# Seven block products instead of eight in the down projections of a two-layer decoder trunk

## The chip, the core and the metric

The kernel runs as one program on one core of a Trainium2 chip. Its time is in device microseconds for one execution; three runs are shown, and their median is the number that is compared. The profile comes from one further execution. Its engines are TensorE (PE, with its weight loads PEld), VectorE (DVE), ScalarE (ACT), GpSimd (POOL) and SyncE (SP, which here issues the loads).

## What is computed

The reference is a trunk of two layers over a residual stream x of 256 tokens by 1024 columns, float32. Each layer has a mixer (attention) and then a feed-forward network (FFN), and a last RMSNorm ends it. The change touches the FFNs alone:

```python
def swiglu(h, w_gate, w_up, w_down):
    return (jax.nn.silu(h @ w_gate) * (h @ w_up)) @ w_down

x = x + swiglu(rmsnorm(x, norm_ffn[layer]), ffn_w_gate[layer], ffn_w_up[layer], ffn_w_down[layer])
```

The gate and up matrices are 1024 x 2816, the down matrix is 2816 x 1024. The down projection multiplies 256 x 2816 values by it.

## The kernel before

**Number format.** Every float32 operand of a matmul is split into a high part, rounded to the format that PE multiplies (fp32r), and a low part, the rest. ACT makes the high part by a copy, DVE the low part by a subtraction. A product is three matmuls: high by high, high by low, low by high (mm3, L361).

**Weights.** The class Weights (L73) holds one queue of all weight tiles in the order of use. A tile of a down projection is one k-tile: 128 rows of the matrix by all 1024 columns, 512 KB. `load` issues its DMA on SP's queue into one of four raw buffers, `prepare` (L98) splits it into one of seven pairs of high and low buffers (L111 on ACT, L114 on DVE), and `next` (L118) hands out a tile and prepares up to six tiles ahead. A split must wait until the matmuls that read the buffer seven tiles earlier are done.

**FFN.** `ffn` (L468) first runs the gate and up projections in eleven chunks of 256 hidden units (L490). A chunk uses four weight tiles, two for the gate and two for the up projection; weights are the stationary operand, the activations of all 256 tokens the moving one (L503 with the weights' high parts, L505 with their low parts). The gate sums lie in two of four PSUM banks with the tag mm, the up sums in the two banks with the tag s, so that the next chunk's up projection needs the banks of the last one. Then, for each of the chunk's two blocks of 128 units (L510 to L520): the gate sums are copied and added, scaled and put through silu in a tile `sg` (three buffers); the up sums are copied to `hn` (L517 on ACT) and added (L518 on DVE), multiplied by `sg` (L519) and split into the tiles `hh` and `hl` (L520, by way of the helper at L247). These hold all 22 k-tiles of hidden values until the down projection ends.

**Down projection.** `residual` (L382) runs over the 22 k-tiles. Here the hidden values are the stationary operand, 128 x 128, and the weights the moving one, 128 x 512. For each k-tile there are two token blocks t by two column halves h, each with three matmuls: 12 matmuls, summed in four banks of tag mm (`ps_out`). The last three k-tiles are kept back and done block by block (L405, L406), so that the first sums are finished early: DVE scales each block by the token's normalization factor and adds it to x (L448), and the next layer's norm (`Norm.half`, L278) multiplies, has PE transpose (L254, in the two banks of tag tp) and splits. In the second layer the final norm follows instead (`Final`, L314).

**Order.** Each engine runs its instructions in an order that is fixed when the program is built: a scheduler goes through them by the order of the source and by when it reckons them ready. SP's loads are held in source order. The next layer's first weight tiles are split during the end of a down projection, in the same queue.

Of the kernel before, what the change touches and what calls it, by code (L numbers as in the profile page):

```python
# [7 lines left out]
F32 = mybir.dt.float32  # L8
# [21 lines left out]
OD_CHUNKS = [304, 256, 512, 512, 512, 512]  # L30
FF_CHUNKS = [256] * 11
WCOLS = 1024


def in_tiles(chunks):
# [37 lines left out]
class Weights:  # L73


    def __init__(self, tc, pool, rpool, flats, specs, ahead, bufs, spare):
        self.tc, self.pool, self.rpool, self.ahead, self.bufs, self.spare = tc, pool, rpool, ahead, bufs, spare
        self.queue = []
        for flat, tiles in zip(flats, specs):
            off = 0  # L80
            for kk, w in tiles:
                n = kk * w
                self.queue.append((flat[off : off + P * n].rearrange("(p c) -> p c", p=P), kk, w))
                off += P * n
        self.raw = []
        self.ready = []
        self.parts = []
        self.used = 0
        self.later = 0

    def load(self, upto):
        while len(self.raw) < min(upto, len(self.queue)):
# [5 lines left out]
    def prepare(self, upto, behind=False):  # L98

        nc = self.tc.nc  # L100
        while len(self.ready) < min(upto, len(self.queue)):
            i = len(self.ready)
            self.load(i + 1)
            raw = self.raw[i]
            self.raw[i] = None
            _, kk, w = self.queue[i]
            n = kk * w
            hi = self.pool.tile([P, WCOLS], F32R, tag="hi", bufs=self.bufs[1], name="w_hi")
            lo = self.pool.tile([P, WCOLS], F32R, tag="lo", bufs=self.bufs[1], name="w_lo")
            with self.tc.high_priority(offset=-self.later):  # L110
                act = nc.scalar.activation(hi[:, :n], raw[:, :n], AF.Copy)  # L111
                if behind:
                    self.tc.keep_in_program_order(act)
                sub = nc.vector.tensor_sub(lo[:, :n], raw[:, :n], hi[:, :n])  # L114
                self.parts.append((act, sub))
            self.ready.append((hi[:, :n].rearrange("p (k c) -> p k c", k=kk), lo[:, :n].rearrange("p (k c) -> p k c", k=kk)))

    def next(self, hold=1):  # L118
        i = self.used
# [7 lines left out]
def trunk(tc, x, w0, w1, sm0, cw, vec, gcol, cst, out, dbg=None):  # L127
# [251 lines left out]
                nm.finish()  # L379
        return ps  # L380

    def residual(act, nk, tail, nxt, rs=None, amid=None, gate=(), hold=False):  # L382

        ps = [[mm_bank("ps_out") for _ in range(2)] for _ in range(NT)]
        inorder = amid is not None and not hold
# [1 line left out]
        def one(t, h, k, wt):  # L387
            c = slice(512 * h, 512 * h + 512)
            skip = isinstance(nxt, Final) and (t, h) == (NT - 1, 1)
            return mm3(ps[t][h], act[t], k, wt[0][:, 0, c], wt[1][:, 0, c], k == 0, k == nk - 1 - skip * tail, skip)  # L390

        for k in range(nk - tail):
            wt = W.next()
            for t in range(NT):
                for h in range(2):
                    one(t, h, k, wt)
        last = [W.next(hold=tail) for _ in range(tail)]
        if amid and not hold:
            order = [(t, h, 0, tail) for t, h in ((0, 0), (0, 1), (1, 0), (1, 1))]
# [68 lines left out]
    def ffn(nm, goff):  # L468
        wide, rs = nm.wide, nm.rs
        nxt = Final() if goff == V_FIN else Norm(goff)  # L470
        with tc.tile_pool(name="ffn", bufs=1, side="left", reuse_waits="tile") as fp:
            hh = fp.tile([P, KF, T], F32R, tag="hh", name="hT_hi")
            hl = fp.tile([P, KF, T], F32R, tag="hl", name="hT_lo")


            ones = fp.tile([P, P], F32, tag="ones", name="ones")
# [13 lines left out]
            for w in FF_CHUNKS:  # L490
# [4 lines left out]
                for dst in (gp, up):  # L495
# [11 lines left out]
                        nm.finish()  # L507
                    if dst is gp and f0 == 0:
                        spread()
                for f in range(nf):  # L510
                    sg = fp.tile([P, T], F32, tag="sg", bufs=3, name="sg")
                    hn = fp.tile([P, T], F32, tag="hn", bufs=3, name="hn")
# [4 lines left out]
                    evac(hn, up[f][:, T:])  # L517
                    V.tensor_add(hn, up[f][:, :T], hn)  # L518
                    V.tensor_mul(hn, hn, sg)  # L519
                    split(hh[:, f0 + f], hl[:, f0 + f], hn)  # L520
                f0 += nf
                if f0 == 3 * nf:
                    gain(goff)
            hT = [[z[:, :, t * P : (t + 1) * P] for z in (hh, hl)] for t in range(NT)]
            residual(hT, KF, 3, nxt, rs)
        return nxt


# [639 lines left out]
```

## Time and profile before

| what | us |
|---|---|
| median of three runs (lowest, highest) | 652.33 (651.77, 652.62) |
| the profiled execution | 652.22 |
| its span, first to last instruction | 650.4 |
| first FFN, first gate matmul in the chain that ended last | 137.97 |
| first FFN, first matmul of the down projection | 261.34 |
| second FFN, first gate matmul in the chain that ended last | 460.06 |
| first split of a down tile that waits for the second down projection's matmuls | 589.00 |

In the page, PE is 88% of the chain that ended last. The three lines of mm3 in the down projections (L363, L364, L365 with `ps_out`) have 176 matmuls each with hidden values as the stationary operand. A matmul's length in the records (389 ns on average for 128 x 512) is longer than the distance of one to the next, since they are pipelined; the distance is read from the starts. A line with a helper's number (L111, L114, L220, L247) collects the calls of many places, so that they are told apart by the names of their tiles and by their shape.

### The profile page before, as it was taken

The numbers are of one execution on the slowest core, as the hardware profiler recorded it, in microseconds if no ns is written. First come the engines' busy times: TensorE is split into PE (matmuls) and PEld (weight loads), VectorE is DVE, ScalarE is ACT, GpSimd is POOL, SyncE is SP. The second block draws the span as 40 slices with busy tenths as digits, with TensorE's granted clock in tenths as the row PEclk, the third lists the DMA queues.
The fourth block names the chain that finished last, engine by engine and source line by source line (L and its number), as shares of the span: only waits on it lengthen the run. The fifth ranks groups of instructions, "written<-read, shape, count | busy, mean of one in ns | idle before, by whom it ended". The sixth has DMA issues, their size and how long they took to land.

```text
span 650.4 us, 10025 instructions
## 1 busy us (share of the span) xinstructions
PE 638.9 (98%) x3521; PEld 537.5 (83%) x3521; DVE 478.9 (74%) x1116; ACT 403.0 (62%) x809; POOL 11.0 (2%) x26
## 2 busy tenths in 40 slices
PE   8999999999999999999999999999999999999995
PEld 5978888888888888888888877776888888888884
DVE  6999976678867677544589889797887777765424
ACT  6685748558665665433377597787676665564314
POOL 2000000100000000000000000000000000000000
PEclk9999999999999999999999999999999999999998
DMA  8834354218755655564186511402286555556501
GB/s 302 295 128 153 98 172 154 97 53 287 244 194 194 193 187 190 183 194 151 49 328 234 188 67 56 171 34 93 85 283 234 190 187 187 183 185 210 191 14 66
DMA packets 31729, 109.02 MB, mean 168 GB/s; under 512 B 3648, under 2 KB 3904, under 8 KB 31424
## 3 DMA queue, kind: packets, MB, share of 16 engines
q1 hardware_dynamic: 31104, 107.79, 49.3%
q10 hardware_dynamic: 576, 0.59, 0.3%
q8 instruction: 28, 0.46, 0.3%
q14 instruction: 21, 0.17, 0.1%
HBM read 107.32 MB, written 1.05 MB: 167 GB/s over the span
## 4 chain that ended last, share of the span: by engine, by line
PE 88%; ACT 4%; DVE 4%; DMA 2%; issue 1%; SPq 0%; POOL 0%; ACTq 0%; DVEq 0%
PE ps_g L503 12%; PE ps_u L503 12%; PE ps_out L364 8%; PE ps_out L365 8%; PE ps_out L363 8%; PE ps_u L505 6%; PE ps_g L505 6%; PE ps_in L364 5%; PE ps_in L365 5%; PE ps_in L363 5%; PE pt_p L998 2%; PE ps_o L1014 2%; PE ps_s L978 1%; DVE w_lo L114 1%; ACT e L466 1%
## 5 line engine op out<-in xcount | busy, mean ns | idle before, releaser
L114 DVE TENSOR_TENSOR w_lo<-w_raw,w_hi 128x1024 fp32r<-128x1024 f32 (+5 forms) x200 | 231.5, 1179 | 112.6 <-ACT w_hi L111 67.7
L111 ACT ACTIVATE w_hi<-w_raw 128x1024 fp32r<-128x1024 f32 (+5 forms) x200 | 203.4, 1025 | 135.5 <-PE ps_out L365 53.4
L503 PE MATMUL ps_u<-aW,w_hi 128*128 128x512 f32 x352 | 84.9, 391 | 0.0
L503 PE MATMUL ps_g<-aW,w_hi 128*128 128x512 f32 x352 | 84.5, 391 | 0.0
L364 PE MATMUL ps_in<-w_lo,aW 128*128 128x512 f32 (+5 forms) x208 | 77.2, 371 | 0.1
L363 PE MATMUL ps_in<-w_hi,aW 128*128 128x512 f32 (+5 forms) x208 | 76.8, 370 | 0.1
L365 PE MATMUL ps_in<-w_hi,aW 128*128 128x512 f32 (+5 forms) x208 | 75.5, 363 | 0.0
L503 PEld LDWEIGHTS ps_g<-aW,w_hi 128*128 128x128 f32 x352 | 64.6, 188 | 13.1 <-DVE aW L247 0.7
L503 PEld LDWEIGHTS ps_u<-aW,w_hi 128*128 128x128 f32 x352 | 64.4, 188 | 12.2
L364 PE MATMUL ps_out<-w_lo,hT_hi 128*128 128x512 f32 (+1 forms) x176 | 68.3, 388 | 0.0
L363 PE MATMUL ps_out<-w_hi,hT_hi 128*128 128x512 f32 (+1 forms) x176 | 68.3, 388 | 0.0
L365 PE MATMUL ps_out<-w_hi,hT_lo 128*128 128x512 f32 (+1 forms) x176 | 68.3, 388 | 0.0
L505 PEld LDWEIGHTS ps_u<-aW,w_lo 128*128 128x128 f32 x352 | 45.4, 191 | 1.9
L505 PEld LDWEIGHTS ps_g<-aW,w_lo 128*128 128x128 f32 x352 | 45.4, 191 | 1.9
L505 PE MATMUL ps_g<-aW,w_lo 128*128 128x256 f32 x352 | 46.0, 283 | 0.0
L505 PE MATMUL ps_u<-aW,w_lo 128*128 128x256 f32 x352 | 46.0, 283 | 0.0
L466 ACT ACTIVATE e<-e,bias 128x128 f32<-128x128 f32 (+1 forms) x96 | 42.4, 446 | 1.3 <-DVE bias L465 0.9
L364 PEld LDWEIGHTS ps_in<-w_lo,aW 128*128 128x128 f32 x208 | 39.3, 189 | 4.6 <-issue 0.5
L363 PEld LDWEIGHTS ps_in<-w_hi,aW 128*128 128x128 f32 x208 | 39.2, 189 | 4.7 <-ACT w_hi L111 0.3
L365 PEld LDWEIGHTS ps_in<-w_hi,aW 128*128 128x128 f32 x208 | 39.2, 188 | 4.6 <-issue 0.5
L365 PEld LDWEIGHTS ps_out<-w_hi,hT_lo 128*128 128x128 f32 x176 | 33.1, 188 | 6.8
L363 PEld LDWEIGHTS ps_out<-w_hi,hT_hi 128*128 128x128 f32 x176 | 33.1, 188 | 6.7
(237 smaller groups left out, 874.7 us busy)
## 6 DMA issues: line engine op xcount, KB each, us to landing
w_raw<-in_w SPq DMA_DIRECT2D x176, 512.0 KB, 3.8
w_raw<-in_w SPq DMA_DIRECT2D x8, 384.0 KB, 4.5
gain<-in_vec SPq DMA_DIRECT2D x4, 512.0 KB, 5.4
cw<-in_cw SPq DMA_DIRECT2D x2, 1024.0 KB, 7.0
w_raw<-in_w SPq DMA_DIRECT2D x4, 416.0 KB, 5.2
w_raw<-in_w SPq DMA_DIRECT2D x4, 328.0 KB, 5.1
w_raw<-in_w SPq DMA_DIRECT2D x4, 304.0 KB, 2.7
x<-in_x SPq DMA_DIRECT2D x4, 256.0 KB, 5.0
```

The costliest lines, as they stand in the source:

```text
L111: act = nc.scalar.activation(hi[:, :n], raw[:, :n], AF.Copy)
L114: sub = nc.vector.tensor_sub(lo[:, :n], raw[:, :n], hi[:, :n])
L363: TE.matmul(ps, act[0][:, k], wh, start=start, stop=False, skip_group_check=skip),
L364: TE.matmul(ps, act[0][:, k], wl, start=False, stop=False, skip_group_check=skip),
L365: TE.matmul(ps, act[1][:, k], wh, start=False, stop=stop, skip_group_check=skip),
L466: return low, A.activation(e, e, AF.Exp, scale=-1.0, bias=bias, accum_out=den)
L503: TE.matmul(dst[f], wt[0][:, i, f * P : (f + 1) * P], wide[:, k].rearrange("p z q -> p (z q)"), start=k == 0, stop=False)
L505: TE.matmul(dst[f][:, :T], wt[1][:, i, f * P : (f + 1) * P], wide[:, k, 0], start=False, stop=k == KD - 1)
L978: mmi = TE.matmul(sb[:, i], qS[t][:, h], kz[:, par, :, :ns], start=z == 0, stop=z == 1)
L998: TE.transpose(pt[:, i, b, st], e[:, i, b, st * P : (st + 1) * P], ident)
L1014: pin(TE.matmul(ob[64 * par : 64 * par + 64], vv[:, st, c : c + 64], pTs[par][:, b, st].rearrange("p j c -> p (j c)"), start=False, stop=l ...
```

## The change

The hidden values and the down weights of two neighbouring k-tiles are taken as a product of two 2 x 2 block matrices: A is two token blocks by two k-tiles, B is two k-tiles by two column halves. In five of the eleven pairs (FAST: pairs 0, 2, 4, 6 and 8) the four result blocks are formed from seven block products instead of eight (the scheme of Strassen and Winograd), each still three matmuls.

- In the gate and up projections, the chunks of these pairs (a chunk of 256 units is a pair) make four sums of blocks of hidden values (`seven_units`), 128 x 128 each, in two tiles of the tag `sg`, and split these and three of the four blocks. `hh` and `hl` grow from 22 x 256 to 7552 columns, and are addressed by a table.
- `Weights.pair` takes two raw tiles, splits three of the four blocks (half of the first tile, all of the second), and makes four differences of 128 x 512 in two raw sum tiles. `Weights.close` splits the two sum tiles into buffers of their own, two for high and two for low parts. For the first pair of a layer this is done at once, in `pair`; for each further one after the matmuls of the pair before it (`seven` calls `W.close()`). A pair is prepared when both of its tiles are within the distance of six.
- `seven` does the 21 matmuls of a pair. Three products go straight into banks of `ps_out`, four into banks of their own: two of tag tp, two of tag s. The fourth bank of `ps_out` gets nothing from the fast pairs.
- After the last fast pair (k-tiles 16 and 17) the four extra sums are combined and added to x, scaled, by one copy on ACT and six operations on DVE, two of them 1024 columns wide. The ordinary k-tiles 18 to 21 follow.

The core of the diff:

```diff
 WCOLS = 1024
+FAST = (0, 2, 4, 6, 8)
...
         self.later = 0
+        self.pairs = {}
+        self.sums = None
+        self.open = None
...
             i = len(self.ready)
+            if i in self.pairs:
+                if i + 2 > upto:
+                    break
+                self.pair(i)
+                continue
             self.load(i + 1)
...
+    def halves(self, hi, lo, src):
+        act = self.tc.nc.scalar.activation(hi, src, AF.Copy)
+        return act, self.tc.nc.vector.tensor_sub(lo, src, hi)
+    def pair(self, i):
+        V = self.tc.nc.vector
+        self.load(i + 2)
+        a, b = self.raw[i : i + 2]
+        self.raw[i : i + 2] = [None] * 2
+        sums = [self.sums.tile([P, WCOLS], F32, tag="ts", bufs=2, name="w_sum") for _ in range(2)]
+        h = slice(0, 512), slice(512, 1024)
+        got = {}
+        for n, (names, src) in enumerate((((("b11",), a), (("b21", "b22"), b)))):
+            hi = self.pool.tile([P, WCOLS], F32R, tag="hi", bufs=self.bufs[1], name="w_hi")
+            lo = self.pool.tile([P, WCOLS], F32R, tag="lo", bufs=self.bufs[1], name="w_lo")
+            c = slice(0, 512 * len(names))
+            self.parts.append(self.halves(hi[:, c], lo[:, c], src[:, c]))
+            for j, name in enumerate(names):
+                got[name] = (hi[:, h[j]], lo[:, h[j]])
+        V.tensor_sub(sums[0][:, h[0]], a[:, h[1]], a[:, h[0]])
+        V.tensor_sub(sums[0][:, h[1]], b[:, h[1]], a[:, h[1]])
+        V.tensor_sub(sums[1][:, h[0]], b[:, h[1]], sums[0][:, h[0]])
+        V.tensor_sub(sums[1][:, h[1]], b[:, h[0]], sums[1][:, h[0]])
+        self.ready += [got, None]
+        if self.open is None:
+            self.open = (got, sums)
+            self.close()
+        else:
+            self.open = (got, sums)
+    def close(self):
+        if self.open:
+            got, sums = self.open
+            for j, names in enumerate((("t1", "t3"), ("t2", "t4"))):
+                hi = self.sums.tile([P, WCOLS], F32R, tag="thi", bufs=2, name="w_shi")
+                lo = self.sums.tile([P, WCOLS], F32R, tag="tlo", bufs=2, name="w_slo")
+                self.halves(hi, lo, sums[j])
+                for n, name in enumerate(names):
+                    c = slice(512 * n, 512 * n + 512)
+                    got[name] = (hi[:, c], lo[:, c])
+            self.open = ()
+    def both(self):
+        i = self.used
+        self.used += 2
+        self.prepare(i + 2 + self.ahead)
+        got = self.ready[i]
+        self.ready[i] = None
+        return got
     def next(self, hold=1):
...
-    def residual(act, nk, tail, nxt, rs=None, amid=None, gate=(), hold=False):
+    def residual(act, nk, tail, nxt, rs=None, amid=None, fast=(), seven=None, gate=(), hold=False):
...
             skip = isinstance(nxt, Final) and (t, h) == (NT - 1, 1)
-            return mm3(ps[t][h], act[t], k, wt[0][:, 0, c], wt[1][:, 0, c], k == 0, k == nk - 1 - skip * tail, skip)
-
-        for k in range(nk - tail):
+            first = 2 * (0 in fast and t == 1 and h == 1)
+            return mm3(ps[t][h], act[t], k, wt[0][:, 0, c], wt[1][:, 0, c], k == first, k == nk - 1 - skip * tail, skip)
+        k = 0
+        while k < nk - tail:
+            if k in fast:
+                seven(ps, k)
+                k += 2
+                continue
             wt = W.next()
             for t in range(NT):
                 for h in range(2):
                     one(t, h, k, wt)
+            k += 1
         last = [W.next(hold=tail) for _ in range(tail)]
...
         with tc.tile_pool(name="ffn", bufs=1, side="left", reuse_waits="tile") as fp:
-            hh = fp.tile([P, KF, T], F32R, tag="hh", name="hT_hi")
-            hl = fp.tile([P, KF, T], F32R, tag="hl", name="hT_lo")
+            at, sums_at, o = {}, {}, 0
+            for k in range(0, KF, 2):
+                if k // 2 in FAST:
+                    at[0, k], at[0, k + 1], at[1, k + 1], sums_at[k] = o, o + P, o + 2 * P, o + 3 * P
+                    o += 7 * P
+                else:
+                    for i in range(2):
+                        for t in range(NT):
+                            at[t, k + i] = o + (NT * i + t) * P
+                    o += 4 * P
+            hh = fp.tile([P, o], F32R, tag="hh", name="hT_hi")
+            hl = fp.tile([P, o], F32R, tag="hl", name="hT_lo")
+            W.sums = fp
+            W.open = None
+            down = W.used + 2 * KD // ff_kk(FF_CHUNKS[0]) * len(FF_CHUNKS)
+            W.pairs = {down + 2 * g for g in FAST}
+            class Units:
+                def __init__(self, z, t):
+                    self.z, self.t = z, t
+                def __getitem__(self, c):
+                    o = at[self.t, c[1]]
+                    return self.z[:, o : o + P]
+            def seven_units(k, hn):
+                ss = [fp.tile([P, 2, P], F32, tag="sg", bufs=3, name="h_sum") for _ in range(2)]
+                a11, a21, a12, a22 = (hn[i][:, t * P : (t + 1) * P] for i in range(2) for t in range(NT))
+                V.tensor_add(ss[0][:, 0], a21, a22)
+                V.tensor_sub(ss[0][:, 1], ss[0][:, 0], a11)
+                V.tensor_sub(ss[1][:, 0], a11, a21)
+                V.tensor_sub(ss[1][:, 1], a12, ss[0][:, 1])
+                o = at[0, k]
+                split(hh[:, o : o + P], hl[:, o : o + P], a11)
+                split(hh[:, o + P : o + 3 * P], hl[:, o + P : o + 3 * P], hn[1])
+                o = sums_at[k]
+                for i in range(2):
+                    c = slice(o + 2 * i * P, o + 2 * (i + 1) * P)
+                    split(hh[:, c], hl[:, c], ss[i].rearrange("p s q -> p (s q)"))
+            made = {}
+            def seven(ps, k):
+                if not made:
+                    for n in (5, 7):
+                        made[n] = t_bank(f"ps_p{n}")
+                    for n in (6, 1):
+                        made[n] = s_bank(f"ps_p{n}")
+                first, last, begin = k == 2 * FAST[0], k == 2 * FAST[-1], k == 0
+                w = W.both()
+                o = sums_at[k]
+                terms = (
+                    (made[5], o, "t1", first, last),
+                    (made[7], o + 2 * P, "t3", first, last),
+                    (ps[1][0], at[1, k + 1], "t4", begin, False),
+                    (made[6], o + P, "t2", first, last),
+                    (made[1], at[0, k], "b11", first, last),
+                    (ps[0][0], at[0, k + 1], "b21", begin, False),
+                    (ps[0][1], o + 3 * P, "b22", begin, False),
+                )
+                for dst, o, name, start, stop in terms:
+                    u = [z[:, o : o + P].unsqueeze(1) for z in (hh, hl)]
+                    mm3(dst, u, 0, *w[name], start, stop)
+                W.close()
+                if last:
+                    ua = W.sums.tile([P, 2, 512], F32, tag="ts", bufs=2, name="c_sum")
+                    ub = W.sums.tile([P, 2, 512], F32, tag="ts", bufs=2, name="c_sum")
+                    evac(ua[:, 0], made[6])
+                    V.tensor_add(ua[:, 0], made[1], ua[:, 0])
+                    V.scalar_tensor_tensor(xs[0][:, :512], made[1], rs[0], xs[0][:, :512], op0=ALU.mult, op1=ALU.add)
+                    V.tensor_add(ua[:, 1], made[5], ua[:, 0])
+                    V.scalar_tensor_tensor(xs[0][:, 512:], ua[:, 1], rs[0], xs[0][:, 512:], op0=ALU.mult, op1=ALU.add)
+                    V.tensor_add(ub, made[7].unsqueeze(1).broadcast_to([P, 2, 512]), ua)
+                    V.scalar_tensor_tensor(xs[1], ub.rearrange("p a c -> p (a c)"), rs[1], xs[1], op0=ALU.mult, op1=ALU.add)
...
                         spread()
+                hns = []
                 for f in range(nf):
...
                     V.tensor_mul(hn, hn, sg)
-                    split(hh[:, f0 + f], hl[:, f0 + f], hn)
+                    hns.append(hn)
+                    if f0 // nf not in FAST:
+                        o = at[0, f0 + f]
+                        split(hh[:, o : o + T], hl[:, o : o + T], hn)
+                    elif f:
+                        seven_units(f0, hns)
                 f0 += nf
                 if f0 == 3 * nf:
                     gain(goff)
-            hT = [[z[:, :, t * P : (t + 1) * P] for z in (hh, hl)] for t in range(NT)]
-            residual(hT, KF, 3, nxt, rs)
+            hT = [[Units(z, t) for z in (hh, hl)] for t in range(NT)]
+            residual(hT, KF, 3, nxt, rs, fast={2 * g for g in FAST}, seven=seven)
         return nxt
```

## The prediction

> **What bounds the kernel now.** I read the page's engine line first, then the clock row, then the busy time by stages of the FFNs, then single instructions where the stages meet. In the stage rows the columns are the stretch, its length, and busy time with instruction counts of PE, PEld, DVE, ACT, POOL; then granted clock and DMA. The first three are gate and up projections of the first FFN (the two of 11.13 us are its last two chunks), the next two its down projection, the last one the down projection of the second.
>
> ```profile
> PE 638.9 (98%) x3521; PEld 537.5 (83%) x3521; DVE 478.9 (74%) x1116; ACT 403.0 (62%) x809; POOL 11.0 (2%) x26
> PEclk9999999999999999999999999999999999999998
> ...
> 161.31:239.24 77.93, 77.93 (x449) 68.89 (x449) 57.81 (x101) 48.26 (x87) 0.00 (x0) 1.00 0.62 203
> 239.24:250.37 11.13, 11.13 (x66) 9.84 (x65) 8.14 (x15) 6.79 (x13) 0.00 (x0) 1.00 0.55 190
> 250.37:261.50 11.13, 11.13 (x66) 9.84 (x65) 8.14 (x15) 6.79 (x13) 0.00 (x0) 1.00 0.56 189
> ...
> 272.40:283.40 11.00, 11.00 (x51) 9.09 (x50) 4.90 (x4) 4.31 (x5) 0.00 (x0) 1.00 0.60 191
> ...
> 305.40:316.00 10.60, 10.60 (x49) 8.77 (x47) 3.87 (x5) 2.55 (x4) 0.00 (x0) 1.00 0.37 106
> 627.40:638.40 11.00, 11.00 (x50) 9.13 (x49) 1.09 (x2) 0.34 (x1) 0.00 (x0) 1.00 0.01 1
> ```
>
> PE is busy 98% of 650.4 us, at the full granted clock, and in each of these stretches it is busy for the whole length: in the FFNs nothing but PE ends last. DVE has 11.13 - 8.14 = 2.99 us free per chunk of the gate and up projections and 11.00 - 4.90 = 6.1 us in 11.00 us of the down projection. So a matmul removed there is worth its spacing, as long as DVE and ACT deliver the operands.
>
> The spacing: a matmul record's own length overlaps the next one, so I take the beat of a whole k-tile (12 matmuls). In the down projection each high-part split waits for PE to free a buffer, and so beats with it.
>
> ```profile
> 589.00 1.06 ACT L111 ACTIVATE w_hi<-w_raw 128x1024 fp32r<-128x1024 f32 x1 [1.30 <-PE ps_out L365]
> 591.72 1.06 ACT L111 ACTIVATE w_hi<-w_raw 128x1024 fp32r<-128x1024 f32 x1 [1.66 <-PE ps_out L365]
> ...
> 624.36 1.06 ACT L111 ACTIVATE w_hi<-w_raw 128x1024 fp32r<-128x1024 f32 x1 [1.66 <-PE ps_out L365]
> ```
>
> From 589.00 to 624.36 there are 13 k-tiles: 35.36 / 13 = 2.72 us each, 2.72 / 12 = 0.2267 us a matmul.
>
> **The change, part by part.**
>
> *Matmuls removed.* A pair of k-tiles has 2 x 4 x 3 = 24 matmuls before and 7 x 3 = 21 after, all of the same 128x512 shape. Five pairs, two layers: 30 matmuls fewer, 30 x 0.2267 = 6.80 us, all of it on PE's path.
>
> The Trainium skill prices this otherwise: its page TensorE: Matmul & The Clock Gate, section Back-to-back issue gap, gives about 131 ns per matmul of 512 columns in a sustained stream with weight loads. By that the saving would be 30 x 0.131 = 3.9 us, as an estimate, and the sum below 2.9 us smaller. The trace does not agree: its beat is 227 ns over 13 k-tiles, and the measurement decides.
>
> *Weight sums and splits, per pair.* The prices:
>
> ```profile
> L114 DVE TENSOR_TENSOR w_lo<-w_raw,w_hi 128x1024 fp32r<-128x1024 f32 x176 | 211.0, 1221 | 100.9 <-ACT w_hi L111 56.0 <-issue 34.1 <-PE ps_g L505 10.5
> L114 DVE TENSOR_TENSOR w_lo<-w_raw,w_hi 128x512 fp32r<-128x512 f32 x4 | 2.6, 684 | 0.0
> L281 DVE TENSOR_TENSOR xg<-x,gain 128x512 f32<-128x512 f32 x12 | 8.3, 690 | 0.3
> L461 DVE TENSOR_TENSOR nb<-nb,rope_b 128x512 f32<-128x512 f32 x4 | 2.7, 680 | 0.0
> L111 ACT ACTIVATE w_hi<-w_raw 128x1024 fp32r<-128x1024 f32 x176 | 185.3, 1059 | 121.6 <-PE ps_out L365 45.7 <-PE ps_u L503 23.4 <-PE ps_g L503 21.5
> L111 ACT ACTIVATE w_hi<-w_raw 128x512 fp32r<-128x512 f32 x4 | 2.3, 618 | 0.0
> ```
>
> DVE before: two low parts, 2 x 1.221 = 2.44 us. After: one low part of half a tile (0.684), one of a tile (1.221), four differences of 128x512 (between L461's 0.680 and L281's 0.690, both two f32 operands: 4 x 0.685 = 2.74), and two low parts of the sum tiles (2.44): 7.09 us, 4.65 more. ACT: 0.618 + 3 x 1.059 = 3.80 instead of 2.12 us. Inside the down projection a fast pair is followed by two ordinary tiles, so the cycle to compare is PE 45 x 0.2267 = 10.20 us, DVE 7.09 + 2.44 = 9.53 us (93%), ACT 3.80 + 2.12 = 5.92 us. On the average nothing takes the bound from PE, but DVE's cover shrinks from 56% to 7%.
>
> The order inside a cycle decides, since the sum tiles have two buffers: the next pair's sums can be split only after the running pair's twelfth matmul (t1, t3, t4 and t2 come first). From there to the next pair's first matmul are 9 + 24 = 33 matmuls, 7.48 us. The chain in this time: three matmuls until b11's buffer is free for the second ordinary tile (0.68), its high part (1.06) and low part (1.22), and the two low parts of the sums (2.44), with their high parts beside them on ACT: 5.40 us. That leaves 2.1 us, so I cost the steady cycle at nothing; the cover is PE's 33 matmuls.
>
> *The loads.* Same bytes in the same order on SP's queue. A pair holds its two raw buffers of four until the differences are done, 2.74 us longer.
>
> ```profile
> w_raw<-in_w SPq DMA_DIRECT2D x176, 512.0 KB, 3.8
> ```
>
> A load lands in 3.8 us, and a pair's buffers were last held by the pair before, one cycle of 10.2 us earlier: nothing, with 6.4 us as cover, of which the longer hold takes 2.74.
>
> *Unit sums in the gate and up projections.* In five chunks a layer DVE gains four 128x128 operations and splits of 128 + 3 x 256 columns for 2 x 256.
>
> ```profile
> L871 DVE TENSOR_TENSOR hw<-hw 128x128 f32<-128x128 f32 x1 | 0.3, 290 | 0.0
> L247 DVE TENSOR_TENSOR hT_lo<-hn,hT_hi 128x256 fp32r<-128x256 f32 x44 | 17.1, 422 | 7.5 <-ACT hT_hi L247 7.4
> ```
>
> At most 4 x 0.29 + 0.29 + 0.42 = 1.87 us of 2.99 us free, behind the additions that empty the banks of the up projection, so no bank waits for it. Nothing, with the weights prepared six tiles ahead as cover.
>
> *The start of the down projection* is where I expect a price. The first pair is prepared whole before the stage begins, the next one's differences right after, and the fourth and fifth products use the two banks that the last up projection has just filled.
>
> ```profile
> 260.64 2.36 DVE L114 TENSOR_TENSOR w_lo<-w_raw,w_hi 128x1024 fp32r<-128x1024 f32 x2 [1.93 <-issue]
> 261.34 0.40 PE L363 MATMUL ps_out<-w_hi,hT_hi 128*128 128x512 f32 x1
> 261.42 0.66 ACT L220 ACTIVATE hn<-ps_u 128x256 f32<-128x256 f32 x2 [0.73 <-PE ps_u L505]
> 262.92 0.75 DVE L518 TENSOR_TENSOR hn<-ps_u,hn 128x256 f32<-128x256 f32 x2
> ```
>
> The stage begins at 261.34. Its tenth matmul (made[6], first bank) is due 9 x 0.2267 = 2.04 us later, at 263.38; the thirteenth (made[1]) at 264.06. The two additions that read these banks now end at 263.34 and 263.67: just in time, so that any delay of DVE goes straight to PE. DVE's extra work due in the last two chunks is 4.65 for the first pair, 0.68 + 2.74 - 1.22 = 2.2 for the second, and 1.87 for the units of the last fast chunk: 8.7 us against 2 x 2.99 = 5.98 us free, 2.7 us too much. Against that, 2.44 us of it are low parts of tiles 2 and 3, due only 4.8 and 7.5 us into the stage, and one of the two low parts that run at 260.64 is now asked for later. The stall lies between 0 and 2.7 us a layer (a gain is excluded: PE has no idle time there to give back). I take 0.6, 1.2 us for both layers, nearer to nothing because the rows of both chunks are rows of free time in which the first pair can be made early. What queues behind a wait of DVE there are the additions, and behind them PE's made[6].
>
> *The sums of the products* (after the last fast pair): two additions, two scaled additions, then one of each over 1024 columns.
>
> ```profile
> L442 DVE TENSOR_TENSOR x<-ps_out,x 128x512 f32<-128x512 f32 x8 | 5.5, 688 | 2.9 <-PE ps_out L365 2.9
> L448 DVE SCALAR_TENSOR_TENSOR x<-ps_out,rs,x 128x512 f32<-128x512 f32 x7 | 5.2, 749 | 13.4 <-PE ps_out L365 13.2
> ...
> L458 DVE SCALAR_TENSOR_TENSOR rope_b<-ps_in,rs,con 128x256 f32<-128x256 f32 x16 | 7.1, 475 | 0.0
> L114 DVE TENSOR_TENSOR w_lo<-w_raw,w_hi 128x608 fp32r<-128x608 f32 x4 | 3.2, 792 | 6.9 <-ACT w_hi L111 6.9
> ```
>
> 2 x 0.688 + 2 x 0.749 + 1.22 + 1.28 (L448 extended by the step from 256 to 512 columns, 0.27 per 256) = 5.4 us. They may start after the pair's fifteenth matmul and must be done before the first L448: 6 + 12 + 9 = 27 matmuls, 6.12 us. In the second layer DVE is free (1.09 of 11.00 us): nothing. In the first, up to three low parts for the next layer (0.79 each) can come between: 7.8 against 6.1, up to 1.7 us late, and behind L448 stand the transposes on PE. Between 0 and 1.7, I take 0.4, because the 305.40 row shows 6.7 of 10.60 us free.
>
> Sum: -6.80 + 1.2 + 0.4 = -5.2 us. The profiled execution took 652.22 us (span 650.4), the median of the runs is 652.33, 0.02% apart; so 652.3 - 5.2 = **647.1 us**.
>
> **The rivals.**
>
> *The meeting points cost their full price* (B): 2 x 2.7 + 1.7 = 7.1 us, 652.6 us, or anything from 648.6 up. For it: the two additions are just in time today, and DVE is over-booked before the start. Against: most of the over-booked work is due later.
>
> *The sums come late in every pair* (C), slower than before. The place: between the twelfth matmul of a fast pair and the first of the next. If the differences and the half low part of the pair after next (2.74 + 0.68) run on DVE ahead of the sums' low parts, the chain of 5.40 becomes 8.82 us against 7.48: PE waits 1.34 us in each of four pairs and two layers, 10.7 us, and the time is 652.3 - 6.8 + 10.7 = 656.2 us. It decides from 6.8 / 8 = 0.85 us a pair, that is 2.9 us of other work ahead of the sums. For it: DVE at 93%, and that at 262.92 an addition whose ACT half was ready by 262.1 starts only as the low parts begun at 260.64 end: DVE keeps its order. Against: that work is asked for later, and its buffers come free later.
>
> The Trainium skill has the rule behind C: TensorE: Matmul & The Clock Gate, section Architectural detail, says that ACT and DVE take their queue strictly in order. By that rule C follows as soon as the order is wrong; the trace agrees on the order, at 262.92.
>
> **How the numbers follow.** Forecast with small stalls 0.61 (its own range 645.3, nothing lost, to 648.6), B 0.24, C 0.15. The range 645.2 to 651.5 leaves out C and B's end. About 0.2%, 1.3 us, is what a measurement of this kernel can tell from no change: 651.0 to 653.6. B reaches it with about a quarter of its chance: faster 0.79, same 0.06, slower 0.15.
>
> **What would show it.** PE with 3491 matmuls instead of 3521 and both down projections some 3 us shorter each. DVE's busy share in the down projection from 45% to over 80%, with little idle time. Step by step: PE waiting at made[6] on DVE's additions near the start (B); PE waiting on sum tiles at each pair's t1 (C); L448 and transposes late at the first layer's end. If the beat of 0.2267 us changes inside a fast pair, or PE stands idle in the gate and up projections, the prediction fails elsewhere than I looked.

## The result

The changed kernel took **645.63 us** (median of 5 runs, 644.73 to 646.79) against 652.62 us for the kernel before beside it; ratio 0.9897, 95% interval 0.9879 to 0.9914. That is 7.0 us faster. The forecast of 647.1 us was 1.5 us longer; the time lies inside its range, near the fast end (645.2). The profiled execution took 644.73 us with a span of 642.9.

The first lines of the page after:

```profile
span 642.9 us, 10156 instructions
PE 631.5 (98%) x3491; PEld 532.0 (83%) x3491; DVE 542.0 (84%) x1248; ACT 423.9 (66%) x851; POOL 11.0 (2%) x26
PEclk9999999999999999999999999999999999999999
```

PE has the 3491 matmuls that were foretold and is busy for the same 98% of a shorter span. DVE has gained 63 us of work (478.9 to 542.0) and sits at 84%.

The busy time by stages, with the columns as in the prediction: the last gate and up chunk, then four cycles of the first layer's down projection (a fast pair and two ordinary tiles each), then the last pair:

```profile
250.00:260.98 10.98, 10.98 (x65) 9.69 (x64) 10.91 (x19) 6.67 (x13) 0.00 (x0) 1.00 0.53 167
260.98:271.20 10.22, 10.22 (x47) 8.46 (x46) 10.19 (x17) 6.54 (x11) 0.00 (x0) 1.00 0.60 189
271.20:281.40 10.20, 10.20 (x46) 8.45 (x45) 10.13 (x13) 5.72 (x6) 0.00 (x0) 1.00 0.70 210
281.40:291.60 10.20, 10.20 (x46) 8.45 (x45) 9.52 (x12) 5.81 (x6) 0.00 (x0) 1.00 0.69 213
291.60:301.80 10.20, 10.20 (x46) 8.45 (x45) 7.58 (x7) 6.24 (x6) 0.00 (x0) 1.00 0.61 183
301.80:312.00 10.20, 10.20 (x46) 8.45 (x45) 7.31 (x10) 3.46 (x5) 0.00 (x0) 1.00 0.38 110
```

A cycle lasts 10.20 us and PE is busy in all of it. The fourth row is a steady cycle: DVE is busy 9.52 us, and 9.53 had been reckoned. In the chunk ahead of the stage and in the first two cycles DVE has nothing free (10.91 of 10.98, 10.19 of 10.22, 10.13 of 10.20). The overbooking that was foretold is there, but PE does not pay for it.

To see where the time went I cut the span at five of PE's matmuls, the same in every run: the first of the gate projection, the first that reads the gate values (down projection begins), the first of ps_h (in the next mixer, behind the input projection), the same first two in the second layer; and at the end of its last down matmul. Each row is the profiled execution of that run, in us:

| run | gate/up 1 | down 1 + input proj. | rest of mixer | gate/up 2 | down 2 | after it |
|---|---|---|---|---|---|---|
| before | 123.53 | 88.08 | 110.48 | 123.43 | 60.14 | 6.93 |
| after | 123.50 | 84.48 | 110.36 | 123.46 | 56.74 | 6.93 |
| two pairs fast | 123.51 | 86.71 | 110.48 | 124.10 | 58.78 | 6.93 |
| banks first | 124.82 | 85.54 | 110.54 | 124.73 | 57.56 | 6.93 |
| first pair not at once | 123.54 | 84.49 | 110.39 | 123.44 | 56.74 | 6.91 |
| last pair reordered | 123.53 | 84.86 | 110.55 | 123.43 | 56.74 | 6.92 |
| one difference twice | 123.54 | 84.77 | 110.42 | 123.45 | 56.98 | 7.00 |
| two differences twice | 123.56 | 88.12 | 110.43 | 123.46 | 58.11 | 6.92 |
| four differences twice | 123.56 | 90.15 | 110.45 | 123.47 | 57.87 | 9.02 |
| one low part twice | 123.57 | 85.16 | 110.50 | 123.44 | 56.74 | 6.93 |
| two low parts twice | 123.55 | 86.59 | 110.62 | 123.43 | 57.00 | 7.53 |
| held longer, no DVE work | 123.55 | 91.72 | 110.41 | 123.46 | 58.49 | 8.52 |
| held much longer | 123.54 | 105.47 | 110.37 | 123.45 | 68.93 | 10.66 |

Down 2 is 3.40 us shorter, which is 15 x 0.2267 to the hundredth. Down 1 with the input projection is 3.60 shorter. Gate and up projections are as before. What is left of the 7.5 us between the two spans (0.33) lies ahead of the first gate matmul, a part that the change does not touch and that varied from 137.0 to 138.6 us over the runs.

The waits of PE between 137 us and 335 us held one entry, in the next layer's input projection; the second layer's down projection had none:

```profile
PE ps_in L426 <- DVE aW L308: 0.4, 1, 0.4
```

### The profile page after: what moved, and what is told of

It reads as the page before. It is cut to its first block, busy times and chain, and to the rows that moved or that the text cites. A ratio compares the mean times of both kernels' runs of the same rounds, so it can differ in the third digit from the quotient of the medians.

```text
span 642.9 us, 10156 instructions
## 1 busy us (share of the span) xinstructions
PE 631.5 (98%) x3491; PEld 532.0 (83%) x3491; DVE 542.0 (84%) x1248; ACT 423.9 (66%) x851; POOL 11.0 (2%) x26
## 4 chain that ended last, share of the span: by engine, by line
PE 90%; ACT 4%; DVE 3%; DMA 1%; issue 1%; POOL 0%; SPq 0%; ACTq 0%; POOLq 0%; DVEq 0%
PE ps_g L645 13%; PE ps_u L645 13%; PE ps_g L647 7%; PE ps_u L647 7%; PE ps_out L426 6%; PE ps_out L425 6%; PE ps_out L424 6%; PE ps_in L426 6%; PE ps_in L424 6%; PE ps_in L425 5%; PE pt_p L1146 2%; PE ps_o L1162 2%; PE ps_s L1126 1%; PE ps_p L425 1%; PE ps_p L424 1%; PE ps_p L426 1%
## 5 line engine op out<-in xcount | busy, mean ns | idle before, releaser
L123 DVE TENSOR_TENSOR w_lo<-w_raw,w_hi 128x1024 fp32r<-128x1024 f32 (+5 forms) x180 | 208.2, 1176 | 51.7 <-ACT w_hi L120 24.3
L120 ACT ACTIVATE w_hi<-w_raw 128x1024 fp32r<-128x1024 f32 (+5 forms) x180 | 182.1, 1020 | 93.5 <-PE ps_g L645 19.8
L426 PE MATMUL ps_out<-w_hi,hT_lo 128*128 128x512 f32 (+1 forms) x116 | 45.0, 388 | 0.0
L424 PE MATMUL ps_out<-w_hi,hT_hi 128*128 128x512 f32 (+1 forms) x116 | 44.9, 387 | 0.0
L425 PE MATMUL ps_out<-w_lo,hT_hi 128*128 128x512 f32 (+1 forms) x116 | 44.9, 387 | 0.0
L424 PEld LDWEIGHTS ps_in<-w_hi,aW 128*128 128x128 f32 x208 | 39.2, 189 | 4.6 <-ACT w_hi L120 0.3
L533 DVE CUSTOM_DVE_ANT_0 e<-ps_s,con 128x128 f32<-128x128 f32 (+1 forms) x80 | 25.3, 351 | 3.4 <-PE ps_s L1126 1.8
L128 ACT ACTIVATE w_hi<-w_raw 128x512 fp32r<-128x512 f32 (+1 forms) x20 | 16.9, 846 | 16.3 <-PE ps_out L426 9.3
```

The source lines that it names most:

```text
L128: act = self.tc.nc.scalar.activation(hi, src, AF.Copy)
L424: TE.matmul(ps, act[0][:, k], wh, start=start, stop=False, skip_group_check=skip),
L425: TE.matmul(ps, act[0][:, k], wl, start=False, stop=False, skip_group_check=skip),
L426: TE.matmul(ps, act[1][:, k], wh, start=False, stop=stop, skip_group_check=skip),
L533: low = V.tensor_tensor_reduce(e, s, m, -scale, 3e38, ALU.add, ALU.min, bias)
```

## The experiments

The stage rows above serve all of them. Ratios are to the kernel before, which took 652.1 to 652.5 us beside them.

**Two pairs in place of five**: is the beat of 0.2267 us the worth of each matmul?

```diff
-FAST = (0, 2, 4, 6, 8)
+FAST = (0, 2)
```

> Only pairs 0 and 2 of each layer by seven products (FAST = (0, 2)); nothing is left out of the result. If a removed matmul is worth its beat of 0.2267 us wherever it stands, 12 matmuls fewer than before give 2.72 us: ratio to before 0.9958, 4.1 us slower than the change. If the gain comes from elsewhere (an earlier start, another order of the work), two pairs keep most of the 7.0 us: ratio near 0.990. If a removed matmul is worth 0.131 us, ratio 0.9976.

Measured 650.36 us, ratio 0.9967 (0.9954 to 0.9980). The interval holds both 0.9958 (12 x 0.2267 us) and 0.9976 (12 x 0.131 us), but the stages decide: down 1 with the input projection is 1.37 us shorter than before and down 2 is 1.36, for 6 matmuls each, and 6 x 0.2267 = 1.36. The page TensorE: Matmul & The Clock Gate of the Trainium skill, section Back-to-back issue gap, would make it 0.79, as an estimate from its 131 ns a matmul; this case does not agree. (Gate and up 2 took 0.6 us more in this run, of which 0.3 is a wait for hn; I have no cause for the rest.)

**Banks first**: the products that use the up projection's banks go to the front (rival B made to happen).

```diff
+                    (made[6], o + P, "t2", first, last),
+                    (made[1], at[0, k], "b11", first, last),
                     (made[5], o, "t1", first, last),
                     (made[7], o + 2 * P, "t3", first, last),
                     (ps[1][0], at[1, k + 1], "t4", begin, False),
-                    (made[6], o + P, "t2", first, last),
-                    (made[1], at[0, k], "b11", first, last),
```

The first pair's matmuls were also kept in this order.

> The first pair's two products into the banks of the up projection (made[6], made[1]) are its first and second instead of its fourth and fifth, and their order is held. Rival B's mechanism (the banks come free just in time): the additions end 1.2 and 2.55 us after the first matmul of the stage in the profile of the change, so PE should wait 1.2 us and then 0.65 us in each layer, 3.8 us in all: ratio near 0.996. If these banks were never near the limit, the time stays at that of the change, 0.990.

Measured 650.16 us, ratio 0.9967 (0.9956 to 0.9979): 4.5 us slower than the change. Two of the three longest entries among PE's waits were

```profile
PE ps_p L424 <- DVE hn L665: 2.2, 2, 1.1
...
PE ps_p L424 <- ACT sg L663: 0.9, 2, 0.5
```

So the meeting point of rival B is real, and its price of 4.5 us is near the 3.8 us expected for this run. What keeps it out of the changed kernel is the order of the products: nine matmuls stand ahead of the first one that needs such a bank.

**First pair not at once**: its sums are split when the second pair is prepared.

```diff
-        if self.open is None:
-            self.open = (got, sums)
-            self.close()
-        else:
-            self.open = (got, sums)
+        self.open = (got, sums)
```

with a close() at the head of pair().

> The sums of the first pair are split when the second pair is prepared, not at once. Two theories. (1) DVE takes its work in the order in which it becomes ready and due, so the place in the program matters little and the first pair's two low parts of sums still run ahead of the down projection's first product: the ratio to the kernel before stays at 0.990 (0.988 to 0.992), the start of both down projections has no wait of PE. (2) The place in the program decides: two low parts of 1.22 us, 2.44 us a layer, move behind the 2.74 us of differences of the second pair, onto the first product's path: 2 x 2.2 to 2 x 2.7 us lost, ratio about 0.997, with PE waiting for the sum tiles at t1 of the first pair.

Measured 645.77 us, ratio 0.9892 (0.9877 to 0.9907), the stages up to the end of down 2 as in the changed kernel within 0.04 us. The part "the first at once" is worth nothing here: the two low parts run at 249.98 and 255.38 us, ahead of the second pair's differences and of the stage's first matmul at 262.18 (in the changed kernel at 248.45 and 250.72, with the first matmul at 260.98), and PE does not wait for them.

**All four differences twice**: 2.74 us more DVE work in each pair, ahead of the sums' low parts (rival C made to happen). The kernel repeats the four subtractions in a loop of two.

> Each pair's four differences are made twice, 2.74 us more of DVE per pair; the result is the same. DVE's free time from the start of the stage to the last fast pair is about 3.6 us in the profile of the change, against 5 x 2.74 = 13.7 us: if DVE's time is what is used up, PE waits some 10 us in each layer, 20 us in all, ratio near 1.02. If the order of the chain (sums late in every pair, rival C) decides, and not the sum of DVE's work, the loss is what exceeds each pair's own margin of 4.7 to 6.3 us, so nothing: ratio near 0.990.

Measured 654.83 us, ratio 1.0038 (1.0022 to 1.0055): 9.2 us slower than the change. Neither number of the expectation was met. PE hardly waited in the down projections; their products came in another order, with ordinary tiles' products drawn ahead of late sum terms, and the delay came out at the end of the first layer:

```profile
PE pt_a L316 <- DVE xg L343: 1.5, 1, 1.5
```

**Two differences twice**: half of that.

> Each pair's first two differences are made twice, 1.37 us more of DVE per pair; the result is the same. By DVE's free time: 5 x 1.37 = 6.85 us against about 3.6 us, so 3.3 us of waiting a layer, 6.5 us in all: ratio near 1.000, the whole gain eaten. By each pair's own margin: nothing, ratio near 0.990.

Measured 650.12 us, ratio 0.9961 (0.9947 to 0.9976): 4.5 us slower than the change, between the two numbers. The place was that of rival C. PE waited for a low part of the sums once in each layer, 1.4 and 0.7 us, at the last fast pair:

```profile
PE ps_p L426 <- DVE w_slo L129: 2.1, 2, 1.4
```

But something else stood behind it. ACT's and DVE's rows in the second layer's down projection:

```profile
605.44 1.06 ACT L128 ACTIVATE w_hi<-w_raw 128x1024 fp32r<-128x1024 f32 x1 [2.79 <-DMA w_raw<-in_w]
```

```profile
606.53 1.23 DVE L129 TENSOR_TENSOR w_lo<-w_raw,w_hi 128x1024 fp32r<-128x1024 f32 x1 [2.26 <-ACT w_hi L128]
```

DVE, the engine with too much to do, stood idle for 2.26 us, since ACT's high part waited 2.79 us for a load. A pair holds its raw tiles until its differences are done, so the doubled differences also delay loads. Two theories were open: DVE's work as such, or the hold of the raw buffers. The next five runs bear on this; how far they part the two is said behind them.

**One difference twice**: the smallest step of both.

```diff
+        V.tensor_sub(sums[0][:, h[0]], a[:, h[1]], a[:, h[0]])
```

> The first of the four differences is made twice: 0.69 us more DVE work in each of 10 pairs, and the raw weights of the pair are held as much longer. If free time of DVE absorbs it (9.52 of 10.2 us busy in a steady cycle, the slack after the sums 4.7 us and more), nothing is lost: ratio 0.990. If each added microsecond costs as in the run with two differences twice (about 4.8 us for 13.7 us added), 2.4 us are lost: ratio 0.9935.

Measured 645.63 us, ratio 0.9894 (0.9879 to 0.9909): nothing lost that the times show (the two stages with the down projections are 0.5 us longer in its profile). The cost is not proportional; there is a slack, and 0.69 us a pair is within it.

**Two low parts of the sums twice**: 2.44 us more DVE work in each pair, and the added subtractions read no raw tile.

```diff
                 self.halves(hi, lo, sums[j])
+                self.tc.nc.vector.tensor_sub(lo, sums[j], hi)
```

> The low parts of the sums are subtracted twice: 2 x 1.22 = 2.44 us more DVE work in each of 10 pairs, nearly as much as the four differences again (2.74 us, 9.3 us lost), but the raw weights are not held any longer by it. If DVE's capacity is the limit (9.53 + 2.44 = 11.97 us in a cycle of 10.20), the loss is like that, 7 to 9 us: ratio 1.001 to 1.003. If the longer hold of the raw buffers and the loads behind it are what counts, the loss is under 4 us: ratio below 0.996.

Measured 649.15 us, ratio 0.9947 (0.9931 to 0.9964): 3.5 us slower than the change, well under the 7 to 9 us of the first theory. The stages of the second layer's down projection, from its second cycle on:

```profile
591.50:601.90 10.40, 10.40 (x47) 8.34 (x46) 10.40 (x13) 4.74 (x5) 0.00 (x0) 1.00 0.44 137
601.90:612.10 10.20, 10.20 (x47) 8.45 (x46) 10.20 (x12) 5.69 (x7) 0.00 (x0) 1.00 0.54 186
612.10:622.30 10.20, 10.20 (x47) 8.45 (x46) 10.20 (x12) 5.47 (x6) 0.00 (x0) 1.00 0.54 191
622.30:632.50 10.20, 10.20 (x46) 8.31 (x45) 10.16 (x12) 2.85 (x4) 0.00 (x0) 1.00 0.13 43
632.50:638.20 5.70, 5.70 (x34) 4.92 (x32) 5.70 (x10) 4.04 (x9) 0.00 (x0) 1.00 0.01 1
```

DVE is full to the last microsecond, and PE still has no gap. A cycle is not closed: what DVE does not get done moves into the tail of the stage, where it had room, and PE takes other products first. That is why 11.97 us of work in cycles of 10.20 cost only 0.26 us in down 2; the first layer, whose tail also splits the next weights, paid 2.1 (this is the fastest execution of the run, 2.8 us above the changed kernel's). The run does not leave the hold alone, though. DVE came later to the differences, so that the loads waited longer for them: SP's waits for w_sum L148, ten in each run, were 50.5 us in all, against 16.7 in the changed kernel.

**One low part of the sums twice**: 1.22 us a pair, nearly the 1.37 us of the two differences.

> One of the two low parts of the sums is subtracted twice: 1.22 us more DVE work in each pair, nearly the 1.37 us of the run with two differences twice (4 to 5 us lost), but with no raw tile held longer. If DVE's work as such cost it there, this loses some 4 us: ratio 0.995. If the hold of the raw tiles, or the place of the work ahead of the sums' splits, cost it, under 1 us: ratio 0.989 to 0.991.

Measured 646.72 us, ratio 0.9911 (0.9895 to 0.9927): about 1 us slower than the change, which is not clear of its noise, where two differences twice cost 4.5. The intervals of these two ratios do not meet, so the amount of DVE work does not set the cost. That the hold stayed the same is not so: SP's waits for w_sum L148 were 39.2 us here. It was only lengthened less than by two differences twice, where the same ten waits (L149 there) were 54.6 us.

**Held longer, no DVE work**: behind the differences of each pair GpSimd makes four small subtractions that read both raw tiles and the last difference.

```diff
+        held = self.sums.tile([P, 16], F32, tag="held", bufs=1, name="held")
+        for src in (a, b, a, b):
+            self.tc.nc.gpsimd.tensor_sub(held, src[:, :16], sums[1][:, 1008:])
```

> Hold alone: behind the four differences of each pair, GpSimd makes 4 small subtractions of 16 columns that read both raw tiles and the last difference, each waiting for the one ahead: the raw buffers come free 1 to 2 us later, and DVE gets no work by it. If the longer hold of the raw buffers (with the loads that wait for them) cost the 4 to 5 us of the run with two differences twice, which held them 1.37 us longer, this loses some 3 to 5 us as well: ratio 0.995 to 0.997, PE waiting for the sum tiles and the second input. If DVE's own work or the order cost it, nothing is lost: ratio 0.989 to 0.990.

Measured 657.29 us, ratio 1.0077 (1.0052 to 1.0103): 11.7 us slower than the change, more than either number. The hold was longer than I had meant, 2.7 to 4.6 us in the five rows of the second layer. One of them, ACT's wait for the load behind it, and the waits of SP's loads for the subtractions:

```profile
612.45 4.56 POOL L153 TENSOR_TENSOR held<-w_raw,w_sum 128x16 f32<-128x16 f32 x4 [5.90 <-issue]
```

```profile
619.79 0.63 ACT L128 ACTIVATE w_hi<-w_raw 128x512 fp32r<-128x512 f32 x1 [4.79 <-DMA w_raw<-in_w]
```

```profile
SPq L99 <- POOL held L153: 53.9, 19, 5.9
```

DVE has no more work than in the changed kernel (541.0 against 542.0 us), and its low parts took the same time (1234 against 1223 ns for w_slo). PE and ACT run the same instructions in the same order as in the changed kernel; on DVE ten in each layer stand at another place. So a longer hold is enough, with no work added on DVE.

**Held much longer**: ten such subtractions in place of four.

> The same with 10 small subtractions in place of 4: the raw buffers are held some 3 to 4 us longer, more than the 2.74 us of the run with all four differences twice. If the hold counts, at least 5 us are lost: ratio 0.997 and above. If not, 0.989 to 0.990; the load of a pair has by the first pairs' rows some 6 us of room, less than 2.74 of it used, so a hold of 4 us is then about at its edge.

Measured 683.34 us, ratio 1.0473 (1.0454 to 1.0492): 37.7 us slower than the change. GpSimd's rows for a whole pair in the second layer were 6.3 to 7.7 us long. PE, ACT and DVE run in exactly the order of the run before, so that nothing but the hold differs. By these rows (which are rough on GpSimd) the ten holds are 24.5 us longer in all than there, and the time is 26 us longer: with the slack gone, each added microsecond of hold costs about one (the lower clock that the waits of PE bring is in this, 0.979 against 0.993 on the mean).

Taken together, the runs do not part DVE's work from the hold: work that DVE does ahead of the differences makes the hold longer too. What orders them is how long ACT, which makes the high parts, waited for the loads of raw tiles in the whole run:

| run | ACT's waits for raw tiles, us | slower than the change, us |
|---|---|---|
| after | 15.2 | 0 |
| one difference twice | 27.1 | 0.0 |
| one low part twice | 30.2 | 1.1 |
| two low parts twice | 35.9 | 3.5 |
| two differences twice | 36.6 | 4.5 |
| four differences twice | 47.5 | 9.2 |
| held longer, no DVE work | 56.2 | 11.7 |
| held much longer | 86.8 | 37.7 |

Two low parts twice and two differences twice have nearly the same waits and nearly the same cost, with 2.44 and 1.37 us of added DVE work a pair. That the waits and the cost go together is not by itself a cause; the cause is shown for the hold alone, by the last two runs.

**Last pair reordered**: t2 and b11 first in the last fast pair, so that the sums of the products may start 2.04 us earlier.

```diff
+                if last:
+                    terms = tuple(terms[i] for i in (3, 4, 0, 1, 2, 5, 6))
```

> In the last fast pair alone, t2 and b11 come first, so the sums of the products may start 6 matmuls after the pair's beginning in place of 15: 9 x 0.2267 = 2.04 us earlier. If the 0.42 us that the first layer's down projection loses (15 matmuls fewer are worth 3.40 us, and the stage got 2.98 us shorter) is lost because these sums end late, the stage from the first down matmul to the second chunk of the next input projection goes from 65.68 to about 65.3 us, the time to about 645.2, and the second layer's stage stays at 56.74. If it is lost elsewhere (the transposes, the next layer's weights), the stage stays at 65.7. The ratio to the kernel before is 0.9890 or 0.9897, too near for the times, so the stage decides.

Measured 645.59 us, ratio 0.9894 (0.9879 to 0.9908): no gain. The stage that the expectation names did come out at 65.28 us, and PE's wait for aW went away. But that mark lies too early: counted to ps_h, where the input projection is over, the stage is 0.38 us longer than in the changed kernel. PE waited later instead:

```profile
PE pt_f L989 <- ACT nk L984: 0.3, 1, 0.3
PE pt_f L989 <- ACT F L281: 0.2, 1, 0.2
```

The 0.42 us that I took for a loss at the first layer's end was no loss; it was a wait that another wait would have taken over. No version beat the change by anything measurable.

## Why the prediction was right, point by point

*Matmuls removed* (-6.80): right. Down 2 lost 3.40 us for 15 matmuls, and the two-pair run gave 1.37 and 1.36 for 6. The two stages together gained 7.00; for the 0.20 above 6.80, all of it in the first layer, no cause is shown.

*The start of the down projection* (+1.2): mis-sized, it cost nothing. DVE's rows at the start, and the two of PE's matmuls that need the banks first:

```profile
260.30 1.23 DVE L129 TENSOR_TENSOR w_lo<-w_raw,w_hi 128x1024 fp32r<-128x1024 f32 x1
...
261.77 0.42 DVE L661 TENSOR_TENSOR hn<-ps_u,hn 128x256 f32<-128x256 f32 x1
...
263.11 0.42 DVE L661 TENSOR_TENSOR hn<-ps_u,hn 128x256 f32<-128x256 f32 x1
263.44 1.22 DVE L123 TENSOR_TENSOR w_lo<-w_raw,w_hi 128x1024 fp32r<-128x1024 f32 x1
```

```profile
263.05 0.39 PE L424 MATMUL ps_p<-w_shi,hT_hi 128*128 128x512 f32 x1
...
263.96 0.39 PE L424 MATMUL ps_p<-w_hi,hT_hi 128*128 128x512 f32 x1
```

One low part runs ahead of the additions where two ran before, and the low parts that are due later follow behind them. The additions end at 262.19 and 263.53; PE asks at 263.05 and 263.96, so 0.86 and 0.43 us are left. One product of a later term (b21) also goes ahead of b11, which gives it 0.23 us. The step that failed is the weight given to the overbooked 2.7 us: nearly all of it was work due later, which the argument named and still priced at 0.6 a layer. The banks-first run shows what the place costs once the additions are due at once.

*The steady cycle* (nothing): right, DVE 9.52 us as reckoned. The slack was better than the 2.1 us of the sum. In the third cycle the low parts of the sums run at

```profile
284.11 1.23 DVE L129 TENSOR_TENSOR w_slo<-w_sum,w_shi 128x1024 fp32r<-128x1024 f32 x1
285.98 1.22 DVE L129 TENSOR_TENSOR w_slo<-w_sum,w_shi 128x1024 fp32r<-128x1024 f32 x1
```

and the first is done at 285.34, with the next pair's first low-part product on PE at

```profile
291.84 0.39 PE L425 MATMUL ps_p<-w_slo,hT_hi 128*128 128x512 f32 x1
```

some 6 us later; the chain had put a whole ordinary tile ahead of them.

*The loads* (nothing): the sum was right, its cover was not. I set 6.4 us against 2.74 of longer hold. That took the buffers as free from the moment of their use. In the second layer, raw tile a of the second pair and its successor in the same buffer:

```profile
584.65 0.62 ACT L128 ACTIVATE w_hi<-w_raw 128x512 fp32r<-128x512 f32 x1
...
594.88 0.62 ACT L128 ACTIVATE w_hi<-w_raw 128x512 fp32r<-128x512 f32 x1
```

```profile
589.83 0.69 DVE L148 TENSOR_TENSOR w_sum<-w_raw 128x512 f32<-128x512 f32 x1
```

```profile
DMA to landing us min/median/max: 3.2/4.2/5.0
```

The hold is 584.65 to 590.52, 5.87 us, and the load 4.2: of a cycle of 10.2 us 0.1 is left, not 3.7. What still covers a later load is the 6 us that the sums have behind it. Five times 0.69 us, 3.4, fits in that; five times 1.37, 6.9, does not. This last reckoning fits the runs with one and two differences twice, and the latter's waits at the last fast pair, but it is an argument; that a longer hold is enough to cost time is shown by the two runs with no DVE work.

*Unit sums in the gate values' buffers* (nothing): right, 123.50 and 123.46 us against 123.53 and 123.43.

*The sums of the products* (+0.4): mis-sized, nothing net. In the first layer they end at 312.52 and L516 follows directly:

```profile
311.24 1.28 DVE L615 SCALAR_TENSOR_TENSOR x<-c_sum,rs,x 128x1024 f32<-128x1024 f32 x1
312.43 0.75 DVE L516 SCALAR_TENSOR_TENSOR x<-ps_out,rs,x 128x512 f32<-128x512 f32 x1
```

PE's one wait of 0.45 us at aW, which went away when they ran earlier, may hang on them, but to the end of the input projection the stage gained 3.60, not less than 3.40.

The two terms that did not come, 1.6 us together, are the difference between the forecast and the measured time: 647.1 - 1.6 = 645.5 against 645.63. Both had been chosen small between nothing and a bound (2.7 a layer, and 1.7), so that the forecast came this near is partly a lucky choice; the term that carries it, the beat of 0.2267 us, is shown. The rivals: B's mechanism is real and is kept off by the order of the terms. C's place is real too, but its rule was too simple: in these runs the cost follows how long the loads of raw tiles are waited for, and what DVE can put off to the stage's end costs little.

## What to carry to other kernels

Price a removed matmul by the beat of its own stage: in the second layer's down projection that held to the hundredth, as no engine that feeds PE fell behind. For a helper engine at 93%, add up its work over the whole stage with its tail, not over one cycle, and set it against what is due first. For each ring of buffers add hold and load and compare with the cycle: here that sum left 0.1 us, and the cost of the runs followed the waits for the loads, whether a busy engine or a mere hold had made them.

## What the runs showed of the hardware

An idle PE can cost more than its idle time. In the run with the longer hold PE stood 3.94 us at the end of the first layer. The stages around it (first column: from, to and length; then PE's busy time; the granted clock is the third number from the end):

```profile
311.00:316.60 5.60, 5.60 (x26) 4.42 (x24) 5.60 (x9) 2.47 (x4) 0.00 (x0) 1.00 0.55 183
316.60:320.70 4.10, 0.16 (x2) 0.03 (x1) 4.07 (x6) 0.00 (x0) 0.00 (x0) 0.96 0.41 125
320.70:324.00 3.30, 3.30 (x12) 2.71 (x13) 1.97 (x3) 1.21 (x3) 0.00 (x0) 0.54 0.00 0
324.00:326.00 2.00, 2.00 (x12) 1.69 (x10) 1.39 (x3) 1.21 (x3) 0.00 (x0) 1.00 0.00 0
```

```profile
322.44 0.63 PE L429 MATMUL ps_out<-w_hi,hT_lo 128*128 128x512 f32 x1
322.87 0.63 PE L427 MATMUL ps_out<-w_hi,hT_hi 128*128 128x512 f32 x1
```

For 3.3 us after the wait the granted clock was 0.54 and matmuls of 512 columns started 0.43 us apart instead of 0.2267: half of that time, some 1.5 us, is lost on top. The Trainium skill, TensorE: Matmul & The Clock Gate, section What's actually happening, says that an idle window of about 3.4 us halves PE's clock until as long a busy one is over; the rows agree. Shorter waits can be followed by a lower clock too. In the run with two differences twice a wait of 1.45 us at the same place left the clock at 1.00, but in the run with all four twice two waits of 1.52 and 0.62 us, 2.5 us apart, were followed by this (its stages of 3 us, from the first wait on):

```profile
319.00:322.00 3.00, 1.44 (x10) 0.81 (x9) 3.00 (x6) 0.30 (x1) 0.21 (x1) 1.00 0.22 80
322.00:325.00 3.00, 2.35 (x12) 1.83 (x11) 3.00 (x6) 3.00 (x8) 0.00 (x0) 0.80 0.00 0
325.00:328.00 3.00, 3.00 (x16) 3.00 (x15) 2.42 (x6) 2.23 (x7) 0.59 (x1) 0.63 0.35 98
```

So a part of the 5.7 us that this run lost in the first layer, by the last two rows at most 3 x 0.20 + 3 x 0.37 = 1.7 us, is PE's clock and not the wait itself.

A subtraction of 16 columns on GpSimd was no small thing: four of them took 2.7 to 5.0 us beside a busy DVE, by the ten rows of the run with the longer hold.
